# Gated delta-rule mixer: decays of a head loaded ahead into four tiles, two tiles for their exponentials, an output row loaded before its gate's projection, and one small scaling on GpSimd

## The chip, the cores and the metric

The kernel runs on one core of a Trainium2 chip. The metric is the device time of one execution in microseconds (us). Before the change three timed runs took 3221.08, 3230.27 and 3230.47 us, median 3230.27 us; a fourth execution was profiled and took 3224.76 us, of which the span from the first to the last instruction is 3221.8 us. About 0.3% is what a measurement of this kernel can tell from no change.

## The reference, cut to what matters

The model has two layers on 1024 tokens of width 1024. Each has a mixer, a cross attention to 256 memory rows and an MLP. The first layer's mixer is mLSTM and stick-breaking attention; the second layer's mixer, the one changed here, is a gated delta rule with 8 heads of width 128:

```python
qkv, gate, b, a = _split(h @ w_in, C_SIZES)
qkv = jax.nn.silu(short_conv(qkv, conv_w))          # 4 taps
q, k = l2norm(q), l2norm(k)
beta = sigmoid(b); log_alpha = -exp(a_log) * softplus(a + dt_bias)
g = cumsum(log_alpha)                               # inside a chunk
decay = where(incl, exp(g[..., :, None] - g[..., None, :]), 0)
lower = where(strict, beta[..., :, None] * kk * decay, 0)
sol = triangular_solve(lower + eye, rhs)
attn = einsum(q, k) * decay
q_dec = q * exp(g)[..., None]
# then a scan over the chunks with a 128x128 state per head
o = rmsnorm(o, head_gain) * silu(gate)
return o.reshape(B, T, GDN_VW) @ w_out
```

The kernel uses chunks of 128 tokens, so each head has 8 chunks, 4 in each half of the sequence.

## The kernel before, in words

Activations lie feature-major, 128 features by 512 tokens a tile, in two halves of the sequence. Every fp32 matrix product is made of three products of the two fp32r parts of each operand (`mm3`, L156 to L158). A weight tile is loaded (`ldw`, L145), cast on ScalarE (ACT, L149), and its rest is taken on GpSimd (POOL, L150).

The program hands its instructions in the order in which the code makes them; a planner then lays down the order of each engine once, before the run, from its own estimates of times, with earlier code first among what is ready. On the chip each engine works off its list in that order, and so does the SP queue, which issues nearly all DMAs: an instruction that waits holds up all that stand behind it on the same engine. A tile with a tag has `bufs` places; a new tile under a tag waits until its place is free. Places named in `mix_start`'s dictionary (`raw`, `kq`, `vc`, `M`, `qe`, `ua`, `kv`) lie in a pool on the right side of the memory that is closed after the last head's preparation. Five places (tag T) hold all short-lived 128x512 tiles made by `tmp`, two (tag P) the staging tiles.

`mix_c` (L819) is the second layer's mixer. It takes the heads in pairs:

- `gdn_head(h)` (L958) projects k, q and v of the head from the layer's input, six products of 24 matmuls each (`take`, evicted on VectorE (DVE) at L431 into `raw`). Head 0 also makes the gates (`c_gates`, L890), which end with the cumulated decays `gr` in HBM (L956).
- `gdn_pre(h, half)` (L987) follows for each half: convolution and SiLU of the three (L1002 to L1008), transposes of k (L1014), sums of squares on ACT (L1017) and PE (L1022, copied at L1023), the norm factors on DVE and POOL (L1024 to L1029, the power on POOL at L1025), the scaled k (L1031), and at L1033 the factors of q, which `gdn_rec` reads much later. At L1035 to L1037 one tile `M` is taken and the decays of this half's four chunks are loaded into it, the same 512 values on all 128 partitions. ACT makes `qe`, their exponential (L1039); POOL multiplies it by q (L1040) and subtracts the mask from M in place (L1042); ACT takes the exponential of each chunk with a bias (L1045). PE makes the products of k with k and q (L1050), DVE scales them by M into `ua` (L1058), PE transposes v (L1071) and DVE scales it (L1073). The five results go to HBM (`put`, L1088, and L1066).
- `gdn_inv` (L1093) inverts the triangular blocks of a pair: loads at L1103, L1122 and L1123, a long run of small DVE instructions (L1109, L1114), then products at L1129 to L1141.
- `gdn_rec` (L1145) is the recurrence over chunks, for pairs up to head 3, and then for the last four heads together. `gdn_out` normalises a half of a head and, for heads 0 to 3, stores it to `od` (L478).

After that, in the code's order, `c_gate(h)` (L871) projects a head's gate, makes its SiLU (L881, L882) in a staging tile `t`, and for the first four heads multiplies it by the stored output: L884 loads that into `e`, the tile that held the tanh, and L885 multiplies. L886 stores the product. Projections of later heads, gates and memory keys fill PE beside the recurrences.

The part around the decays, in the code before:

```python
M = self.keep("M", dt=F32)
m3 = M.rearrange("p (c t) -> p c t", c=4)
nc.sync.dma_start(out=m3, in_=self.gr[c4, h].partition_broadcast(128))
qe = self.keep("qe", dt=F32)
nc.scalar.activation(qe, M, AF.Exp)
nc.gpsimd.tensor_mul(qe, qe, kq[:, 1])
```

Of the kernel before, what the change touches and what calls it, by code (L numbers as in the profile page):

```python
# [11 lines left out]
F32 = mybir.dt.float32  # L12
# [10 lines left out]
HALVES = (0, 1)  # L23
# [3 lines left out]
class Model:  # L27
# [336 lines left out]
    def mix(self, l):  # L364
        if l == 0:
            with self.phase(
                dict(z=3, so=1, ml=2),
                **dict(kq=8, v=4, e=2, sp=2, sh=2, sl=1, wh=2, wl=1, A=2, ah=1, al=1, so_st=1),
            ):
                self.mix_start(l, "so", dict(M=3, W=2, V=2, N=4, C=1, st=1, gg=1, ot=1))  # L370
                self.mix_ab()
                self.out_parts(False)
                self.x_open(self.x_src)
                self.out_proj(self.a["ab_o"])
        else:
            with self.phase(
                dict(a=2, i=1, rec=2, o=1),
                **dict(X=3, Y=2, Uk=1, pr=1, B=4, y=3, S=4, on=2),
            ):
                self.first = [self.ldw(self.a["c_w"][i]) for i in (8, 0)]  # L380
                self.mix_start(l, "o", dict(raw=5, kq=2, vc=1, M=1, qe=1, ua=1, kv=2))
                self.mix_c()
                self.out_parts(True)
                self.x_open(self.x_src, (1,))
                self.out_proj(self.a["c_o"])
# [214 lines left out]
    def ml_heads(self, p):  # L600
        nc = self.nc
        C = None
        for half in HALVES:
# [3 lines left out]
            for i in range(4):  # L607
# [3 lines left out]

                t = self.keep("M", 512, F32)
                qd, k, q = t[:, :256], t[:, 256:384], t[:, 384:]
                t = self.keep("M", 512, F32)
                vT, d = t[:, :256], t[:, 256:]
# [255 lines left out]
    def c_gate(self, h):  # L871

        nc = self.nc

        def gate(i, w, half):
            cols = slice(half * 512, half * 512 + 512)
            t, e = self.stage(), self.tmp()
            ps = self.proj(w, half)
            with self.tc.high_priority():
                self.scaled(t, ps, half)  # L880
            nc.scalar.activation(e, t, AF.Tanh, scale=0.5)  # L881
            nc.vector.scalar_tensor_tensor(out=t, in0=e, scalar=1.0, in1=t, op0=ALU.add, op1=ALU.mult)  # L882
            if h < 4:
                nc.sync.dma_start(out=e, in_=self.od[h][:, cols])  # L884
                nc.vector.tensor_mul(t, t, e)  # L885
            nc.sync.dma_start(out=self.pj[i][:, cols], in_=t)  # L886

        self.lagged([24 + h], lambda i: self.ldw(self.a["c_w"][i]), gate)
# [69 lines left out]
    def gdn_head(self, h):  # L958

        nc = self.nc  # L960
        raw = {}

        def take(i, w, half):
            t = self.ph2("raw", [128, 515])
            ps = self.proj(w, half)
            with self.tc.high_priority():
                self.scaled(t[:, 3:515], ps, half)
                if half == 0:
                    nc.gpsimd.memset(t[:, 0:3], 0.0)
                else:  # L970
                    nc.gpsimd.tensor_copy(t[:, 0:3], raw[i, 0][:, 512:515])
            raw[i, half] = t
            if (i, half) == (16, 0):
                self.c_gates()

        ld = lambda i: self.first.pop(0) if self.first else self.ldw(self.a["c_w"][i])
        self.lagged((8 + h, h, 16 + h), ld, take, 2 if h == 0 else 1)
        oq = self.cols([128, 8])
        for half in HALVES:
            self.gdn_pre(h, half, [raw[i, half] for i in (8 + h, h, 16 + h)], oq)  # L980
        return oq

    def ph2(self, tag, shape):
        pool = self.pr if tag in self.right else self.ph
        return pool.tile(list(shape), F32, tag=tag, name=self.nm(tag), bufs=self.bufs[tag])

    def gdn_pre(self, h, half, raws, oq):  # L987

        nc = self.nc
        mm = nc.tensor.matmul
        chunks = [slice(i * 128, i * 128 + 128) for i in range(4)]
        c4 = slice(4 * half, 4 * half + 4)
        kq = self.ph2("kq", [128, 2, 512])
        vc = self.keep("vc", dt=F32)
        for tl, raw, dst in zip((8 + h, h, 16 + h), raws, (kq[:, 0], kq[:, 1], vc)):
            cv = self.tmp()  # L1000
            wj = lambda j: self.convw[:, tl * 4 + j : tl * 4 + j + 1]
            nc.scalar.mul(cv, raw[:, 0:512], wj(0))  # L1002
            for j in range(1, 4):
                nc.vector.scalar_tensor_tensor(  # L1004
                    out=cv, in0=raw[:, j : j + 512], scalar=wj(j), in1=cv, op0=ALU.mult, op1=ALU.add
                )
            nc.scalar.activation(dst, cv, AF.Tanh, scale=0.5)
            nc.vector.scalar_tensor_tensor(out=dst, in0=dst, scalar=1.0, in1=cv, op0=ALU.add, op1=ALU.mult)  # L1008
        self.put(h, half, 0, kq[:, 0])

        ss, r, c = (self.small([128, 8]) for _ in range(3))
        pk = self.bank("a")
        for s in chunks:
            nc.tensor.transpose(out=pk[:, s], in_=kq[:, 0, s], identity=self.ident)  # L1014
        kt = self.keep("kv", dt=F32)
        for i, s in enumerate(chunks):
            nc.scalar.activation(kt[:, s], pk[:, s], AF.Square, accum_out=ss[:, i : i + 1])  # L1017
        pn = self.bank("a")
        sq = self.tmp()
        nc.scalar.activation(sq, kq[:, 1], AF.Square)  # L1020
        for i, s in enumerate(chunks):
            mm(pn[:, i : i + 1], sq[:, s], self.ones[:, 0:1], start=True, stop=True)  # L1022
        nc.vector.tensor_copy(ss[:, 4:8], pn[:, 0:4])  # L1023
        nc.vector.tensor_scalar(out=ss, in0=ss, scalar1=0.25, scalar2=EPS, op0=ALU.mult, op1=ALU.add)  # L1024
        nc.gpsimd.tensor_tensor(out=r, in0=ss, in1=self.power, op=ALU.pow)  # L1025
        nc.vector.reciprocal(c[:, 0:4], ss[:, 0:4])
        nc.vector.tensor_mul(c[:, 0:4], c[:, 0:4], self.gcol("beta", h, half))
        kd = c[:, 4:8]
        nc.vector.tensor_mul(kd, c[:, 0:4], self.gcol("ed", h, half))  # L1029
        for i, s in enumerate(chunks):  # L1030
            nc.scalar.mul(kt[:, s], pk[:, s], kd[:, i : i + 1])  # L1031
        self.put(h, half, 3, kt)
        nc.vector.tensor_scalar_mul(oq[:, c4], r[:, 4:8], 0.5 * 128.0**-0.5)  # L1033

        M = self.keep("M", dt=F32)  # L1035
        m3 = M.rearrange("p (c t) -> p c t", c=4)
        nc.sync.dma_start(out=m3, in_=self.gr[c4, h].partition_broadcast(128))  # L1037
        qe = self.keep("qe", dt=F32)
        nc.scalar.activation(qe, M, AF.Exp)  # L1039
        nc.gpsimd.tensor_mul(qe, qe, kq[:, 1])  # L1040
        self.put(h, half, 1, qe)
        nc.gpsimd.tensor_sub(m3, m3, self.mask_a.unsqueeze(1).broadcast_to([128, 4, 128]))  # L1042
        ng = self.gcol("ng", h, half)
        for i in range(4):
            nc.scalar.activation(m3[:, i], m3[:, i], AF.Exp, bias=ng[:, i : i + 1])  # L1045
        ua = self.ph2("ua", [128, 4, 2, 128])
        for i in range(0, 4, 2):
            p = self.bank("a")
            for j in range(2):
                mm(  # L1050
                    p[:, j * 256 : j * 256 + 256].rearrange("p (n t) -> p n t", n=2),
                    kq[:, 0, chunks[i + j]],
                    kq[:, :, chunks[i + j]],
                    start=True,
                    stop=True,
                )
            for j in range(2):
                nc.vector.scalar_tensor_tensor(  # L1058
                    out=ua[:, i + j],
                    in0=p[:, j * 256 : j * 256 + 256].rearrange("p (n t) -> p n t", n=2),  # L1060
                    scalar=c[:, i + j : i + j + 1],
                    in1=m3[:, i + j].unsqueeze(1).broadcast_to([128, 2, 128]),
                    op0=ALU.mult,
                    op1=ALU.mult,
                )
        nc.sync.dma_start(out=self.dense(self.Ud[h])[:, c4], in_=ua[:, :, 0])  # L1066
        self.put(h, half, 2, ua[:, :, 1])

        p = self.bank("a")
        for s in chunks:  # L1070
            nc.tensor.transpose(out=p[:, s], in_=vc[:, s], identity=self.ident)  # L1071
        t = self.keep("kv", dt=F32)
        nc.vector.tensor_mul(  # L1073
            t.rearrange("p (c d) -> p c d", c=4),
            p.rearrange("p (c d) -> p c d", c=4),
            r[:, 0:4].unsqueeze(2).broadcast_to([128, 4, 128]),
        )
        self.put(h, half, 4, t)
# [692 lines left out]
```

## Time and profile before

| what | value |
|---|---|
| timed runs, median (lowest to highest) | 3230.27 us (3221.08 to 3230.47) |
| the profiled execution | 3224.76 us |
| its span | 3221.8 us |
| mean granted TensorE clock | 0.971 |
| PE busy | 3045.2 us, 95% |
| DVE busy | 2115.9 us, 66% |
| ACT busy | 1330.2 us, 41% |
| POOL busy | 945.4 us, 29% |
| DMA | 438.04 MB, mean 136 GB/s |

PE is TensorE's matrix products, DVE is VectorE, ACT is ScalarE, POOL is GpSimd, SP the queue that issues DMAs. "Busy" is the time in which an engine executes an instruction. A wait is put down to what released it last. TensorE's clock has two levels, 1.2 and 2.4 GHz; a granted clock of 1.00 is 2.4 GHz throughout, 0.50 is 1.2 GHz. The stage of the second mixer's head preparations, inversions and first recurrences lies between 1520 and 2010 us of the span, the last recurrences and the gates after it.

### The profile page before, as it was taken

What the parts mean: (1) busy time and instruction counts of PE and PEld (TensorE: products, weight loads), DVE (VectorE), ACT (ScalarE), POOL (GpSimd) and SP (SyncE); (2) the same over time, 40 slices, a digit from 0 to 9 for tenths busy, and PEclk for the clock granted to TensorE, in tenths of its full rate; (3) what the DMA queues carried; (4) which work ended last, traced back from release to release, by engine and by line L of the source; (5) the groups of instructions that cost most, each with busy time, mean ns of one, the idle gap of its engine ahead of it and who ended that gap; (6) DMA issues with size and microseconds to landing.
All of it is one profiled execution on the core that took longest, in us unless ns stands there. A gap on an engine that the chain in (4) does not pass through costs nothing.

```text
span 3221.8 us, 39997 instructions
## 1 busy us (share of the span) xinstructions
PE 3045.2 (95%) x14447; PEld 2511.5 (78%) x14447; DVE 2115.9 (66%) x3342; ACT 1330.2 (41%) x2525; POOL 945.4 (29%) x725
## 2 busy tenths in 40 slices
PE   8999989999899999998988899899999899999997
PEld 6777777888678878887777788788888678878886
DVE  5567475545786667777777775654454786667777
ACT  3254464424354454433443333234333354444442
POOL 2354565313000032234343333125323100023323
PEclk9999989999899999999999899999999999999998
DMA  4333553213244464443345556665212234474432
GB/s 151 109 119 103 156 175 119 70 39 102 75 143 157 152 238 167 147 164 100 87 117 142 149 156 187 191 231 187 66 56 77 97 111 149 157 250 173 148 144 79
DMA packets 268374, 438.04 MB, mean 136 GB/s; under 512 B 38064, under 2 KB 146832, under 8 KB 261008
## 3 DMA queue, kind: packets, MB, share of 16 engines
q1 hardware_dynamic: 268176, 435.50, 41.4%
q8 instruction: 113, 1.85, 0.2%
q14 instruction: 85, 0.70, 0.1%
HBM read 300.60 MB, written 134.81 MB: 135 GB/s over the span
## 4 chain that ended last, share of the span: by engine, by line
PE 33%; DVE 9%; DMA 4%; issue 4%; POOL 1%; ACT 1%; SPq 0%; POOLq 0%; DVEq 0%; ACTq 0%
PE mm L158 3%; PE mm L157 3%; PE mm L156 3%; PE ga L1453 2%; PE ga L1454 2%; PE ga L1455 2%; PE gb L1454 1%; DVE t L1004 1%; PE gb L1455 1%; PE gb L1453 1%; PE gc L1454 1%; PE gc L1455 1%; PE gc L1453 1%; PE mm L1454 1%; PE mm L1455 1%
## 5 line engine op out<-in xcount | busy, mean ns | idle before, releaser
L156 PE MATMUL mm<-hh,wh 128*128 128x512 f32 x1248 | 503.4, 404 | 8.2 <-DVE raw L431 3.5
L157 PE MATMUL mm<-hl,wh 128*128 128x512 f32 x1248 | 504.3, 404 | 0.0
L158 PE MATMUL mm<-hh,wl 128*128 128x512 f32 x1248 | 501.9, 402 | 0.0
L150 POOL TENSOR_TENSOR wl<-wr,wh 128x1024 fp32r<-128x1024 f32 x128 | 320.6, 2506 | 448.8 <-ACT wh L149 423.4
L1445 POOL TENSOR_TENSOR r<-r,r 128x512 f32<-128x512 f32 x64 | 92.0, 1458 | 881.8 <-DVE lo L1412 881.8
L1412 DVE TENSOR_TENSOR lo<-r,hi 128x1024 fp32r<-128x1024 f32 x192 | 252.8, 1317 | 133.1 <-ACT hi L1411 132.3
L1411 ACT CAST hi<-r 128x1024 fp32r<-128x1024 f32 x192 | 201.6, 1051 | 313.7 <-PE mm L1454 126.6
L156 PEld LDWEIGHTS mm<-hh,wh 128*128 128x128 f32 x1248 | 239.4, 192 | 59.2 <-DVE raw L431 4.8
L158 PEld LDWEIGHTS mm<-hh,wl 128*128 128x128 f32 x1248 | 240.5, 193 | 48.3 <-issue 0.9
L157 PEld LDWEIGHTS mm<-hl,wh 128*128 128x128 f32 x1248 | 240.2, 192 | 48.0 <-DVE hl L474 0.4
L149 ACT CAST wh<-wr 128x1024 fp32r<-128x1024 f32 x128 | 133.8, 1046 | 213.2 <-PE mm L157 120.8
L1412 DVE TENSOR_TENSOR lo<-br,hi 128x512 fp32r<-128x512 f32 x224 | 187.0, 852 | 32.9 <-ACT hi L1411 32.8
L1453 PE MATMUL ga<-hi,hi 128*128 128x512 f32 x528 | 206.7, 392 | 1.8 <-ACT w L1550 1.0
L1455 PE MATMUL ga<-hi,lo 128*128 128x512 f32 x528 | 206.5, 391 | 0.0
L1454 PE MATMUL ga<-lo,hi 128*128 128x512 f32 x528 | 206.5, 391 | 0.0
L1411 ACT CAST hi<-br 128x512 fp32r<-128x512 f32 x224 | 133.4, 619 | 152.0 <-PE ga L1455 90.0
L1454 PE MATMUL gb<-lo,hi 128*128 128x512 f32 x432 | 169.8, 393 | 7.6 <-DVE lo L1412 7.6
L1453 PE MATMUL gb<-hi,hi 128*128 128x512 f32 x432 | 169.8, 394 | 3.6 <-ACT hi L1411 3.1
L1454 PE MATMUL gc<-lo,hi 128*128 128x512 f32 x432 | 169.1, 391 | 2.3 <-DVE lo L1412 2.3
L1455 PE MATMUL gb<-hi,lo 128*128 128x512 f32 x432 | 169.0, 392 | 0.0
L1455 PE MATMUL gc<-hi,lo 128*128 128x512 f32 x432 | 168.2, 390 | 0.0
L1453 PE MATMUL gc<-hi,hi 128*128 128x512 f32 x432 | 167.8, 390 | 0.0
(515 smaller groups left out, 7228.5 us busy)
## 6 DMA issues: line engine op xcount, KB each, us to landing
r<-in_w SPq DMA_DIRECT2D x128, 512.0 KB, 4.2
br<-hd SPq DMA_DIRECT2D x56, 1024.0 KB, 5.4
hd<-w SPq DMA_DIRECT2D x160, 256.0 KB, 3.1
B<-Bd SPq DMA_DIRECT2D x64, 384.0 KB, 4.5
hd<-t SPq DMA_DIRECT2D x64, 256.0 KB, 5.2
wr<-in_c_w SPq DMA_DIRECT2D x32, 512.0 KB, 4.3
wr<-in_ab_w SPq DMA_DIRECT2D x24, 512.0 KB, 3.6
pj<-p SPq DMA_DIRECT2D x48, 256.0 KB, 2.1
```

What stands on the lines that cost most here:

```text
L149: nc.scalar.copy(hi, raw)
L150: (eng or nc.gpsimd).tensor_sub(lo, raw, hi.bitcast(F32))
L156: mm(out, w[0], x[0], start=first, stop=False)
L157: mm(out, w[0], x[1], start=False, stop=False)
L158: return mm(out, w[1], x[0], start=False, stop=last)
L1004: nc.vector.scalar_tensor_tensor(out=cv, in0=raw[:, j : j + 512], scalar=wj(j), in1=cv, op0=ALU.mult, op1=ALU.add)
L1411: nc.scalar.copy(hi, src)
L1412: (eng or nc.vector).tensor_sub(lo, src, hi.bitcast(F32))
L1445: self.nc.gpsimd.tensor_add(out[:, i : i + 512], a[:, i : i + 512], b[:, i : i + 512])
L1453: mm(ps, hi, b[k][0], start=first and k == 0, stop=False, skip_group_check=True)
L1454: mm(ps, hi, b[k][1], start=False, stop=False, skip_group_check=True)
L1455: mm(ps, lo, b[k][0], start=False, stop=last and k == 3, skip_group_check=True)
```

## The change

Four things are changed, all in the second mixer. The tile M has 4 places instead of 1 and qe has 2 instead of 1. A new function loads both halves' decays of a head; for heads 1 to 7 it stands at the head's start, ahead of its projections, and for head 0 behind them, since the gates are made there. `gdn_pre` is given its tile and loads nothing. The scaling at L1033 moves from DVE to POOL. In `c_gate` the stored output is loaded into a T tile of its own, ahead of the projection.

```diff
-  self.mix_start(l, "o", dict(raw=5, kq=2, vc=1, M=1, qe=1, ua=1, kv=2))
+  self.mix_start(l, "o", dict(raw=5, kq=2, vc=1, M=4, qe=2, ua=1, kv=2))
...
   def gate(i, w, half):
       t, e = self.stage(), self.tmp()
+      if h < 4:
+          o = self.tmp()
+          nc.sync.dma_start(out=o, in_=self.od[h][:, cols])
       ps = self.proj(w, half)
...
       if h < 4:
-          nc.sync.dma_start(out=e, in_=self.od[h][:, cols])
-          nc.vector.tensor_mul(t, t, e)
+          nc.vector.tensor_mul(t, t, o)
...
   def gdn_head(self, h):
+      if h > 0:
+          M = self.decays(h)
...
       self.lagged((8 + h, h, 16 + h), ld, take, 2 if h == 0 else 1)
+      if h == 0:
+          M = self.decays(h)
       for half in HALVES:
-          self.gdn_pre(h, half, [raw[i, half] for i in (8 + h, h, 16 + h)], oq)
+          self.gdn_pre(h, half, [raw[i, half] for i in (8 + h, h, 16 + h)], oq, M[half])
...
+  def decays(self, h):
+      tiles = []
+      for half in HALVES:
+          tiles.append(self.keep("M", dt=F32))
+          self.nc.sync.dma_start(
+              out=tiles[half].rearrange("p (c t) -> p c t", c=4),
+              in_=self.gr[4 * half : 4 * half + 4, h].partition_broadcast(128),
+          )
+      return tiles
...
-      nc.vector.tensor_scalar_mul(oq[:, c4], r[:, 4:8], 0.5 * 128.0**-0.5)
-      M = self.keep("M", dt=F32)
+      nc.gpsimd.tensor_scalar_mul(oq[:, c4], r[:, 4:8], 0.5 * 128.0**-0.5)
       m3 = M.rearrange("p (c t) -> p c t", c=4)
-      nc.sync.dma_start(out=m3, in_=self.gr[c4, h].partition_broadcast(128))
```

## Rows read from the trace of the kernel before

**Rows 1.** The page, its span and its part 1, busy time of each engine.

```profile
span 3221.8 us, 39997 instructions
...
PE 3045.2 (95%) x14447; PEld 2511.5 (78%) x14447; DVE 2115.9 (66%) x3342; ACT 1330.2 (41%) x2525; POOL 945.4 (29%) x725
```

**Rows 2.** Windows by stage: length, busy per engine (instructions), then granted clock, DMA share, GB/s.

```profile
1520.00:2010.00 490.00, 446.05 (x2334) 373.21 (x2333) 355.21 (x724) 192.20 (x509) 165.31 (x137) 0.95 0.49 136
2010.00:2150.00 140.00, 127.37 (x707) 109.12 (x706) 82.73 (x188) 42.96 (x112) 24.79 (x15) 0.95 0.63 204
```

**Rows 3.** PE's waits, 1530 to 2010 us: in total, times, longest.

```profile
PE a L1050 <- DVE s L1023: 6.6, 4, 3.2
PE a L1050 <- ACT kv L1031: 4.5, 5, 2.5
...
PE a L1071 <- DVE ua L1058: 2.8, 1, 2.8
PE mm L156 <- DVE s L1027: 2.3, 1, 2.3
PE a L1050 <- DVE ua L1058: 2.0, 1, 2.0
...
PE a L1014 <- DVE ua L1058: 0.9, 1, 0.9
```

**Rows 4.** Waits of the other engines, 1530 to 2010 us.

```profile
ACT qe L1039 <- DMA M<-gr: 101.2, 16, 13.0
...
DVE c L1033 <- POOL s L1025: 9.4, 7, 4.2
```

**Rows 5.** Timelines of SP, ACT, DVE and PE around one gap: start, length, and idle before it.

```profile
1626.05 0.74 SPq L1037 DMA_DIRECT2D M<-gr  x1
...
1632.90 0.63 ACT L1039 ACTIVATE qe<-M 128x512 f32<-128x512 f32 x1 [4.60 <-DMA M<-gr]
...
1634.59 0.39 DVE L1024 TENSOR_SCALAR s<-s 128x8 f32<-128x8 f32 x1 [2.76 <-ACT kv L1017]
...
1645.87 0.48 PE L1071 MATMUL a<-ident,vc 128*128 128x128 f32 x1 [2.77 <-DVE ua L1058]
```

**Rows 6.** Windows: one gap (the second row), four stretches behind gaps; columns of rows 2.

```profile
1597.40:1601.20 3.80, 3.80 (x10) 3.03 (x11) 3.18 (x8) 3.22 (x8) 3.13 (x3) 0.55 0.00 0
1642.90:1645.60 2.70, 0.20 (x1) 0.00 (x0) 2.66 (x4) 0.00 (x0) 0.83 (x2) 0.97 0.35 137
1645.60:1649.00 3.40, 3.13 (x10) 2.67 (x11) 2.55 (x6) 2.28 (x4) 0.00 (x0) 0.52 0.00 0
...
1662.70:1666.00 3.30, 3.20 (x8) 2.54 (x9) 3.27 (x15) 0.96 (x4) 1.81 (x3) 0.51 0.01 2
...
1716.30:1720.60 4.30, 3.89 (x10) 2.72 (x11) 4.27 (x12) 3.07 (x7) 1.93 (x4) 0.60 0.21 61
```

**Rows 7.** The load of the decays, L1037: length on SP, first and last start; time to landing.

```profile
L1037 SPq DMA_DIRECT2D M<-gr x16: 383/556/2418, 1555.6 to 1976.8; - x16
...
DMA to landing us min/median/max: 4.7/6.8/8.8
```

**Rows 8.** ACT's timeline at the first head's first half.

```profile
1560.35 0.63 ACT L1039 ACTIVATE qe<-M 128x512 f32<-128x512 f32 x1 [6.07 <-DMA M<-gr]
```

**Rows 9.** Windows: the whole machine between 1580 and 1720 us; columns as in rows 2.

```profile
1580.00:1720.00 140.00, 123.20 (x550) 97.98 (x549) 116.56 (x214) 58.20 (x153) 53.60 (x46) 0.95 0.44 120
```

**Rows 10.** Groups by line, 1530 to 2010 us: busy, mean ns, idle before.

```profile
L1033 DVE TENSOR_SCALAR c<-s 128x4 f32<-128x4 f32 x16 | 8.7, 546 | 11.6 <-POOL s L1025 9.4 <-POOL raw L969 2.2
```

**Rows 11.** Two small POOL operations by line: shortest, median and longest in ns.

```profile
L971 POOL COPY raw<-raw x24: 178/186/691, 1523.7 to 1950.5; 128x3 f32<-128x3 f32 x24
...
L1206 POOL TENSOR_TENSOR s<-s,mhalf x16: 1006/1007/2553, 1879.9 to 2197.9; 128x4 f32<-128x4 f32 x16
```

**Rows 12.** Waits around the gates, 1960 to 2240 us.

```profile
DVE p L885 <- DMA t<-od: 7.0, 6, 2.8
...
DVE p L431 <- DMA pc<-p: 6.5, 3, 4.4
```

More of the change, by code (lines that the diff above doesn't have):

```diff
@@ L985, in ph2, with gdn_pre @@
         return pool.tile(list(shape), F32, tag=tag, name=self.nm(tag), bufs=self.bufs[tag])
-    def gdn_pre(self, h, half, raws, oq):
+    def gdn_pre(self, h, half, raws, oq, M):
         nc = self.nc
```

## The prediction

> **What bounds the kernel now.** I read the page first. PE is busy for 3045.2 of 3221.8 us [rows 1], so whatever the change does elsewhere, it can give back only PE's idle time and the time that PE worked at the lower clock. The windows by stage come next. In the stage of the changed code, 1520 to 2010 us, PE is busy for 446.05 of 490 us at a granted clock of 0.95; behind it, up to 2150 us, for 127.37 of 140 us [rows 2]. So the stage holds 44 us of idle PE and at most another 0.05 x 490 = 24 us of clock. No other engine is full: DVE is busy 355.21 us and ACT 192.20 us of the 490.
>
> PE's own waits tell which part of the 44 us can belong to the change. Six kinds end in work of the head preparation: 6.6 + 4.5 + 2.8 + 2.3 + 2.0 + 0.9 = 19.1 us in 13 waits [rows 3]. The rest belongs to inversions, recurrences and short gaps, which the change doesn't touch directly. The releasers named are DVE and ACT, so I looked at what those waited for. ACT's largest wait is for the load of the decays, 101.2 us in 16 waits, one at each half of each head [rows 4].
>
> One gap shows how the one leads to the other [rows 5]. SP issues the load at 1626.05 us. ACT stands still for 4.60 us until 1632.90. The sums of squares (L1017) stand behind that exponential on ACT, so DVE waits 2.76 us for them before L1024, and everything behind it on DVE comes in a heap: eleven microseconds later PE waits 2.77 us for DVE's `ua`, and during that gap DVE is busy for 2.66 of 2.70 us [rows 6]. Six of the thirteen waits, the long ones, have this pattern of a late load, a standing ACT and then a crowded DVE. Why the load is late is in the code and in its row: there is one tile M, so the load of a half can start only when DVE's L1058 has finished the half before, and from there it takes 4.7 to 8.8 us, median 6.8, to land [rows 7].
>
> A gap costs more than its length. Behind four of these gaps PE worked at the lower level of its clock: granted 0.55, 0.52, 0.51 and 0.60 over 3.8, 3.4, 3.3 and 4.3 us [rows 6], a loss of 1.7 + 1.6 + 1.6 + 1.7 = 6.7 us by length times the missing share.
>
> **The change part by part.** *The decays ahead.* The 16 loads stay, with the same bytes and 16 x 0.56 = 9 us on SP [rows 7]. They move, past the weight loads of the head's projections on SP and past every `put` of the preparation, to the head's start; a place in M is free then, because four places hold two heads and the head before the last has long been finished. They wait for nothing new, except that the first two wait for `gr` as the first one does now. Ahead of a head's preparation PE has 6 x 24 = 144 matmuls, at 446.05 / 2334 = 0.19 us an instruction of this stage [rows 2] some 27 us, three times the longest landing; so the load has landed when ACT comes to it, from head 1 on, and in head 0's second half. The first wait stays, 6.07 us [rows 8]; it costs PE nothing. So about 95 of ACT's 101.2 us go. What PE can get of that is at most the 19.1 us of waits and 6.7 us of clock, 25.8 us, and at least nothing. What is late next is DVE. Between 1580 and 1720 us PE is busy 123.20 and DVE 116.56 of 140 us [rows 9]; if all of PE's 16.8 idle microseconds went, the stretch would last 123 us and DVE would be busy for 95% of it, too much for none of PE's waits to be left. I take somewhat under two thirds, 16 us, since the waits of the pattern are the long ones and all four clock losses follow them.
>
> The Trainium skill ("DMA: Bandwidth & Descriptors", "Anatomy of one DMA") speaks against so large a term: it gives a fixed cost of about 2 us and bytes at 436 GB/s beside it, by which, as an estimate, 256 KB would land in 2.6 us; two thirds of ACT's wait would not exist and the term would be near 5 us. That fit is for DMAs issued from GpSimd, and this load is SP's; the measured 6.8 us [rows 7] decide here.
>
> *The second qe tile.* ACT's next exponential no longer waits for the store of the last. Counted at zero: the halves lie far enough apart, and the store stays hidden under the next half's convolution; without that cover it would be part of ACT's wait above, which is not counted twice.
>
> *The scaling on POOL.* DVE loses 16 instructions, 8.7 us busy, and the 11.6 us for which it stood in front of them until POOL's power was ready [rows 10]: 20.3 us off the engine that is late next. It is what makes the 16 us above believable, and gives PE nothing by itself, as PE never waits for L1033. On POOL the new instruction stands directly behind the power that it reads. Its duration there is not in the trace: 0.19 us is the median of a 128x3 copy, 1.01 us that of a 128x4 power [rows 11], so 3 to 16 us of a stage in which POOL is busy for 165.31 of 490 us [rows 2]. I take the copy's, as a multiplication by a constant is nearest to it. Behind it on POOL wait qe and the masks, by at most 1 us a half. Should POOL hold up DVE while it runs, the upper end would take back most of DVE's gain; that is in the range.
>
> *The output ahead of the gate.* The load no longer waits for the tanh and the product, which both use its tile, and DVE no longer waits for it: 7.0 us in 6 waits before L885 [rows 12]. PE sees little of that. I take 1 us, between 7 us and a loss: the tile is one more of five T places, held over a projection, and if the gates had to wait for places as they now do for staging tiles, that would be another 6.5 us [rows 12] the wrong way.
>
> **The sum.** 16 + 1 = 17 us off the profiled execution's 3224.76 us makes 3207.8 us. The three runs lie from 3.7 us below to 5.7 us above that execution, 2.5 us above it on average, so I predict 3210 us.
>
> **The rivals.** *DVE takes the place (0.18).* The ACT wait goes, but DVE's heap stays, because its work and POOL's stay; PE's gaps keep their number and lose a third of their 19.1 us, the clock drops stay: 6 us gained, 3221 us. For it: DVE is full in the gap [rows 6] and 83% busy around it [rows 9]. Against it: DVE loses 20.3 us and its own wait for ACT.
>
> *PE is put in front of DVE (0.15).* The place is PE's order at L1050, L1071 and L1014. The planner now sees the decays ready early, draws the preparation closer together and puts these products earlier between the projections, where DVE, which runs behind the plan, isn't ready. Each such wait costs about 2 us and 1.7 us of clock [rows 3, 6]. The change loses as soon as there are more of them than the long ones that it removes. With five more long ones than now it is 5 x 3.7 = 18 us slower, 3245 us with the 2.5 us. For it: DVE is the next engine. Against it: it is lightened at the same time.
>
> *The loads don't come earlier on the chip (0.07).* SP works in the planner's order; if the loads stood there behind waiting `put`s, ACT would wait as now, and the time stays near 3227 us. Against it: they stand ahead of the head's projections in the code, and earlier code goes first.
>
> **How the numbers follow.** The forecast has 0.60: nearly all of it is faster by over 0.3%, that is below 3220.6 us. About 0.3% is what a measurement of this kernel can tell from no change. The first and third rivals are no change, 0.18 + 0.07 = 0.25; the second is slower, 0.15. The low end takes the whole 25.8 us and the gates' 7 us, 3224.76 - 32.8 + 2.5 = 3194 us. The high end takes in the two rivals without change and the milder half of the slower one, 3236 us.
>
> **What would show it.** Right: ACT's wait before qe falls from 101.2 to under 15 us; DVE has no wait for the power before a scaling; PE's idle time between 1520 us and the end of the last preparation falls by some 10 us, its waits for the preparation from 19.1 to near 8 us, and one or two fewer stretches at the lower clock stand behind them. Wrong: ACT still waits for M; or it doesn't, and PE's waits at L1050 and L1071 are as many as before; or new waits of PE for recurrences or inversions take their place.

## The result and the profile after

The changed kernel takes 3209.80 us (median of 5 runs, 3203.43 to 3212.15), the kernel before beside it 3229.96 us (median of 5, 3221.08 to 3230.47). The ratio is 0.9943, with a 95% interval of 0.9928 to 0.9958: it is faster, by 18 us of the 3230 as the ratio has it. The profiled execution took 3212.15 us.

The page of the changed kernel, span and part 1, answers to [rows 1]:

```profile
span 3210.4 us, 39963 instructions
...
PE 3036.4 (95%) x14447; PEld 2504.0 (78%) x14447; DVE 2117.5 (66%) x3326; ACT 1332.3 (41%) x2525; POOL 955.1 (30%) x741
```

PE does the same 14447 products in 9 us less busy time (3045.2 us before [rows 1]). For the stages, windows of equal content are better than windows of equal time. The stage of the preparations runs from the end of the gates to the end of the last preparation, 1552 to 2008 us before and 1553 to 1985 us after; then the last inversion, the last recurrences, and the output projection to its end. The kernel before (columns as in [rows 2]):

```profile
1552.00:2008.00 456.00, 414.01 (x2181) 349.71 (x2180) 347.36 (x700) 181.59 (x492) 159.26 (x132) 0.94 0.52 144
2008.00:2116.00 108.00, 99.16 (x550) 85.10 (x549) 61.18 (x136) 25.46 (x61) 18.29 (x11) 0.95 0.56 177
...
1552.00:2320.00 768.00, 708.39 (x3800) 603.02 (x3799) 507.27 (x1017) 294.30 (x745) 264.56 (x190) 0.96 0.53 156
```

The changed kernel, the same stages:

```profile
1553.00:1985.00 432.00, 398.40 (x2127) 335.93 (x2127) 346.52 (x676) 178.69 (x481) 164.25 (x146) 0.96 0.55 149
1985.00:2073.00 88.00, 82.45 (x507) 73.11 (x506) 54.77 (x133) 23.12 (x64) 17.00 (x11) 0.96 0.61 192
...
1553.00:2301.00 748.00, 699.02 (x3798) 594.45 (x3798) 509.38 (x1001) 294.87 (x744) 272.79 (x206) 0.97 0.55 160
```

The mixer as a whole is 20 us shorter, 748 against 768. About half of that is idle PE, 59.6 before (768 - 708.39) and 49.0 after; the other half is the same products (3800 and 3798 recorded) in 9.4 us less, at a granted clock of 0.97 instead of 0.96. The preparations end 24 us sooner after the gates (456 to 432 us) and the last inversion takes 20 us less (108 to 88 us); the work that PE then still has to do takes 24 us more, 228 against 204 us. Outside the mixer the two profiled executions differ the other way, 3221.8 - 768 = 2453.8 us before and 3210.4 - 748 = 2462.4 us after, which is why they lie only 12.6 us apart. Most of that, 7 us, lies behind the mixer, and there it is the profile of the kernel before that is short: its last 3848 products, to the end of the span, take 902.0 us, where the other thirteen profiles of this document have 903.5 to 908.9 us. The mixer itself repeats far better: 768 us in the profile before and in those of two kernels below that gained nothing (the extra memset; the scaling last on DVE).

ACT's waits before the exponential, and the new ones of GpSimd, 1530 to 2010 us of the changed kernel (its L1054 is L1039 of before, L1055 is L1040, L1057 is L1042):

```profile
POOL qe L1055 <- DVE kq L1025: 59.0, 12, 11.2
...
POOL M L1057 <- ACT qe L1054: 45.8, 12, 9.2
ACT qe L1054 <- DMA Bd<-qe: 40.3, 10, 9.8
...
ACT qe L1054 <- DMA M<-gr: 8.5, 2, 6.8
```

The wait for the load has gone from 101.2 us in 16 waits [rows 4] to 8.5 us in 2. A new one stands in its place: ACT waits 40.3 us for a qe tile to be stored, and GpSimd's mask waits 45.8 us behind ACT. GpSimd's wait for this exponential isn't new in itself; before, its product with q (L1040) stood there for longer, in the same window:

```profile
POOL qe L1040 <- ACT qe L1039: 104.3, 8, 23.7
```

In the new order ACT makes the exponential ahead of its use. Its 7th, at 1642.21 us, waits for the store, issued at 1635.50 us, of the 5th qe tile, two halves back; the half whose products PE made just then was the 4th.

PE's waits in the stage of the preparations, changed kernel (L1065, L1086, L1039, L1031 and L1144 are L1050, L1071, L1022, L1014 and L1129 of before):

```profile
PE a L1065 <- ACT kv L1048: 6.7, 5, 2.0
PE i L1144 <- DMA X<-Xd: 6.2, 2, 5.1
PE a L1086 <- DVE ua L1073: 5.7, 3, 3.2
PE rec L1186 <- DVE S L1200: 2.7, 1, 2.7
PE a L1039 <- ACT t L1037: 2.4, 1, 2.4
PE a L1039 <- DVE kv L1088: 2.2, 3, 1.5
PE a L1031 <- DVE ua L1073: 2.0, 2, 1.5
PE a L1065 <- DVE s L1040: 1.4, 1, 1.4
```

Those of the preparation listed here are 6.7 + 5.7 + 2.4 + 2.2 + 2.0 + 1.4 = 20.4 us, against 19.1 us before [rows 3]. The gain is not there.

Where it is shows when the stage is cut in two, at the end of DVE's scaling of the fourth head (L1058, L1073 in the changed kernel). The kernel before, heads 0 to 3 and heads 4 to 7:

```profile
1552.00:1750.00 198.00, 178.05 (x808) 143.93 (x807) 162.79 (x290) 82.67 (x214) 75.86 (x64) 0.95 0.44 118
1750.00:2008.00 258.00, 235.96 (x1375) 205.78 (x1374) 184.56 (x411) 98.92 (x279) 83.39 (x68) 0.94 0.58 164
```

The changed kernel:

```profile
1553.00:1750.00 197.00, 175.18 (x789) 140.51 (x789) 160.47 (x278) 85.94 (x225) 87.75 (x76) 0.96 0.47 124
1750.00:1985.00 235.00, 223.22 (x1339) 195.42 (x1338) 186.04 (x399) 92.75 (x257) 76.50 (x70) 0.97 0.62 169
```

The first four heads, in which the prediction read its gap, gain nothing: 198 and 197 us, though ACT's waits for the load there fell from 42.4 to 8.5 us. All of the gain is in the last four, where PE's idle time falls from 22.0 to 11.8 us and the granted clock rises from 0.94 to 0.97. Of PE's waits there the preparation had only 3.0 us before; it has 0.6 us after. The others, of the inversions and recurrences, fell from 18.7 to 10.9 us.

### The profile page after: what moved, and what is told of

It reads as the page before. It is cut to its first block, busy times and chain, and to the rows that moved or that the text cites. A ratio compares the mean times of both kernels' runs of the same rounds, so it can differ in the third digit from the quotient of the medians.

```text
span 3210.4 us, 39963 instructions
## 1 busy us (share of the span) xinstructions
PE 3036.4 (95%) x14447; PEld 2504.0 (78%) x14447; DVE 2117.5 (66%) x3326; ACT 1332.3 (41%) x2525; POOL 955.1 (30%) x741
```

## The experiments

All were timed in five rounds beside runs of the kernel before on the same chip. Medians of the kernel before were 3224.73, 3224.77, 3225.21 and 3230.68 us in the four groups of experiments and 3229.96 us beside the changed kernel, so ratios are compared and not times. A ratio here isn't the quotient of two medians; the two differ by up to 0.0015, or 5 us (two places each: 0.9901 by the medians), and kernels are told apart no more finely than by their intervals.

| kernel | median us | ratio to before | 95% interval |
|---|---|---|---|
| changed kernel | 3209.80 | 0.9943 | 0.9928 to 0.9958 |
| decays alone | 3214.84 | 0.9963 | 0.9946 to 0.9980 |
| gate alone | 3215.04 | 0.9969 | 0.9954 to 0.9984 |
| scaling alone | 3214.03 | 0.9966 | 0.9952 to 0.9980 |
| changed, one qe tile | 3207.39 | 0.9934 | 0.9915 to 0.9953 |
| before, extra memset | 3223.37 | 0.9997 | 0.9985 to 1.0010 |
| before, scaling last on DVE | 3221.80 | 0.9993 | 0.9980 to 1.0006 |
| before, own tile for the stored output | 3231.83 | 1.0027 | 1.0016 to 1.0038 |
| changed, loads behind the projections | 3204.82 | 0.9940 | 0.9926 to 0.9954 |
| changed, two places for M | 3209.41 | 0.9950 | 0.9933 to 0.9967 |
| changed, one load for all heads | 3190.88 | 0.9896 | 0.9880 to 0.9913 |
| changed, mask in a tile of its own | 3197.24 | 0.9920 | 0.9906 to 0.9935 |
| changed, two places each | 3198.71 | 0.9916 | 0.9891 to 0.9940 |

### Each part alone

**The decays alone.** The gate and the scaling as before:

```diff
-  self.mix_start(l, "o", dict(raw=5, kq=2, vc=1, M=1, qe=1, ua=1, kv=2))
+  self.mix_start(l, "o", dict(raw=5, kq=2, vc=1, M=4, qe=2, ua=1, kv=2))
...
+      if h > 0:
+          M = self.decays(h)
```

> Of the change the decays' part alone: four M tiles, two qe tiles, both loads at the head's start; the scaling stays on VectorE and the gate's load where it was. Theory (the late load of the decays is the cause): ACT's wait for that load falls from 101.2 us to under 15 us and most of the gain is here, some 13 to 20 us below the kernel before (ratio 0.994 to 0.996). Rival (the gain is the scaling's, which frees VectorE, or the gates'): under 6 us gained, ratio above 0.998, though ACT's wait for the load is gone just the same.

Measured: 0.9963, or 12 us. ACT's wait for the load is 9.7 us in 2 waits. Alone, the decays give 12 of the change's 18 us, a little less than expected, and the rival's 6 us lie at the end of the interval. The preparations take 429 us in place of 456, and 14 of these 27 us go again behind them (326 us in place of 312). PE's waits for the preparation stay here as well, 17.2 us in its stage of preparations (1550 to 1979 us): the late load was not what they hung on.

**The gate alone.**

```diff
+  if h < 4:
+      o = self.tmp()
+      nc.sync.dma_start(out=o, in_=self.od[h][:, cols])
   ps = self.proj(w, half)
...
-      nc.sync.dma_start(out=e, in_=self.od[h][:, cols])
-      nc.vector.tensor_mul(t, t, e)
+      nc.vector.tensor_mul(t, t, o)
```

> The gate's part alone: the stored output is loaded into a tile of its own ahead of the gate's projection, all else as before. Theory: VectorE's 7.0 us of waits before the multiplication go, TensorE gets about 1 us, ratio 0.998 to 1.002. Rival (the gates and the end of the mixer carry the gain): 5 us or more, ratio below 0.9985.

Measured: 0.9969, 10 us; the rival. The profiled mixer is 14 us shorter. 8 us of that lie in the stage of the preparations (448 against 456 us), some 3 us of them before 1924 us (the end of DVE's scaling of the 14th half), ahead of the first gate's load at 1955 us. The other 6 us lie behind it. What changes there is seen in SP's own waits, between the end of the last preparation and the end of the last inversion. The kernel before, 2008 to 2116 us:

```profile
SPq L886 <- DVE p L882: 16.2, 4, 7.3
SPq L886 <- DVE X L1114: 10.5, 2, 5.4
...
SPq L884 <- DVE X L1114: 9.0, 2, 6.1
...
SPq L884 <- DVE pr L1109: 5.6, 2, 5.2
SPq L886 <- DVE p L885: 4.5, 2, 3.4
...
SPq L884 <- DMA od<-on: 3.2, 2, 2.2
SPq L886 <- DVE pr L1109: 2.7, 2, 1.4
```

The kernel with the gate's part alone, 1998 to 2087 us (L888 is L886 of before, the store of the gate; L880 is the load):

```profile
SPq L888 <- DVE p L885: 8.3, 3, 4.4
SPq L888 <- DVE p L887: 4.9, 2, 2.7
SPq L888 <- DVE pr L1111: 4.9, 2, 4.3
...
SPq L888 <- DVE X L1116: 3.4, 1, 3.4
...
SPq L880 <- DMA od<-on: 1.6, 1, 1.6
...
SPq L880 <- DMA B<-Bd: 1.1, 1, 1.1
```

Before, SP stood 51.7 us of this stage's 108 in front of a gate's load or store, 17.8 us of it at the loads (L884); with the load ahead it is 24.2 us of 89 by these rows, 2.7 us at the loads (L880). Behind such a waiting DMA on SP stand the loads of the inversion and of the recurrences. SP as a whole is no freer for it: all its waits together take 82 of 108 us before and 68 of 89 us here, 76% both times, and the last experiment of the next section takes as much from the gates' standing without a gain. That the gain comes by SP is argued, not shown. The stage is shorter by 19 us. Part of its filling work is only put off (500 products against 550); up to the end of the output projection the gate's part alone takes 306 us where the kernel before takes 312 (its row stands further down), with PE idle for 13.8 us instead of 17.6 us:

```profile
1998.00:2304.00 306.00, 292.21 (x1623) 251.41 (x1622) 157.60 (x319) 112.26 (x254) 105.30 (x58) 0.98 0.55 175
```

**The scaling alone.**

```diff
-  nc.vector.tensor_scalar_mul(oq[:, c4], r[:, 4:8], 0.5 * 128.0**-0.5)
+  nc.gpsimd.tensor_scalar_mul(oq[:, c4], r[:, 4:8], 0.5 * 128.0**-0.5)
```

> The scaling's part alone: the 128x4 scaling on GpSimd, all else as before. Theory: VectorE loses 20 us of work and waiting, but what TensorE waits for is behind the late load, so the time stays, ratio 0.998 to 1.002. Rival (VectorE is what holds TensorE): 5 us or more gained, ratio below 0.9985. If a new order of the instructions alone moves the time by several us, it shows here too, in either direction.

Measured: 0.9966, 11 us; the rival again. The instruction itself, scaling alone:

```profile
L1033 POOL TENSOR_SCALAR c<-s x16: 229/240/699, 1575.2 to 1986.3; 128x4 f32<-128x4 f32 x16
```

0.24 us on GpSimd is the median; on DVE it is 0.17 us. The mean of 0.55 us [rows 10] comes of a few long ones, up to 3.31 us; of the 8.7 us that the prediction counts as DVE's work, 16 times the median is 2.7 us. DVE's standing of 11.6 us before it [rows 10] is gone. The preparations take 445 us (1549 to 1994) in place of 456, but PE's waits for them stay, 19.4 us.

The three parts alone give 12, 10 and 11 us by their ratios, 33 us together; the change with all three gives 18. They overlap.

### Is it the edit, or any new order?

Three parts of like size, two of them far beyond their working, could be one accident: the planner lays down a new order after any edit. An edit that should do nothing was tried, and two that take a part of the change to pieces.

**An extra memset.** Behind the scaling:

```diff
+  nc.gpsimd.memset(self.small([128, 4], "N"), 0.0)
```

> The kernel before with one small GpSimd memset of 128x4 added in each half's preparation, behind the scaling, which stays on VectorE: GpSimd's side of the moved scaling without VectorE's relief. Theory (each part of the change has its own effect): the time stays or is up to 5 us longer, ratio 0.999 to 1.002. Rival (each part alone gained 10 us only because any edit makes the planner lay out the mixer anew, and the order before is an unlucky one): again some 10 us faster, ratio near 0.9967.

Measured: 0.9997, no change. The stage of the preparations came out as before, 456 us with PE busy 413.56 us:

```profile
1546.00:2002.00 456.00, 413.56 (x2181) 348.89 (x2180) 350.05 (x701) 181.39 (x492) 159.87 (x132) 0.94 0.52 144
```

So not every edit gives 10 us, and one small instruction more on GpSimd costs nothing (unlike the scaling there, it waits for no input). But this edit left the stage nearly as it was; it says little on what an edit that does move the order gives by luck.

**The scaling last, on DVE.**

```diff
-  nc.vector.tensor_scalar_mul(oq[:, c4], r[:, 4:8], 0.5 * 128.0**-0.5)
...
   self.put(h, half, 4, t)
+  nc.vector.tensor_scalar_mul(oq[:, c4], r[:, 4:8], 0.5 * 128.0**-0.5)
```

> The kernel before with the scaling left on VectorE but moved to the end of the preparation, so that VectorE no longer stands before it until the power is ready. Theory (the standing is what the scaling's move took away, not its 2.7 us of work): VectorE's 9.4 us of waits for the power go and the time falls as with the move to GpSimd, 8 to 12 us, ratio near 0.9967. Rival (the relief is in the work or in the new order): under 4 us.

Measured: 0.9993, no change; but the standing it was meant to remove stayed:

```profile
L1078 DVE TENSOR_SCALAR c<-s x16: 149/170/3327, 1568.3 to 1983.9; 128x4 f32<-128x4 f32 x16
...
  POOL s L1025: 10.7, 6
```

DVE still stood 10.7 us for the power in front of the scaling: the planner had put it nearly where it was. The run doesn't tell standing from work, and that question stays open. That a kernel in which DVE wasn't relieved gained nothing fits a gain by DVE's relief, and fits a gain by order alone as well.

**Own tile for the stored output, the load where it was.**

```diff
   if h < 4:
-      nc.sync.dma_start(out=e, in_=self.od[h][:, cols])
-      nc.vector.tensor_mul(t, t, e)
+      o = self.tmp()
+      nc.sync.dma_start(out=o, in_=self.od[h][:, cols])
+      nc.vector.tensor_mul(t, t, o)
```

> The kernel before with the stored output loaded into a tile of its own, the load standing where it stood, behind the gate's SiLU in the code. Theory (in the gate's part the gain is that the load no longer waits on SP for the product that read its tile, so that SP is free for the loads behind it): the planner can place the load early and most of the 10 us of the gate's part are here. Rival (the place in the code, ahead of the projection, is what matters): under 4 us gained.

Measured: 1.0027, slower, by 9 us. The extra tile alone is no gain. The loss is a clock loss. From the end of the last preparation to the end of the output projection, kernel before:

```profile
2008.00:2320.00 312.00, 294.38 (x1621) 253.31 (x1620) 159.91 (x318) 112.71 (x253) 105.30 (x58) 0.97 0.54 174
```

and with the tile of its own:

```profile
2001.00:2322.00 321.00, 306.94 (x1621) 265.49 (x1620) 160.91 (x318) 112.17 (x253) 105.29 (x58) 0.93 0.51 168
```

PE is idle for less, 14.1 against 17.6 us, and yet needs 12.6 us more for the same 1621 products, at a granted clock of 0.93 instead of 0.97. The timed executions agree: the mean granted clock of the twelve is 0.9698, that of the kernel before beside them 0.9715. The loss lies in one stretch of the last inversion; two rows of PE's timeline and a window:

```profile
2047.91 3.44 PE L1130 MATMUL i<-X,Uk 128*128 128x64 f32 x16 [2.68 <-DMA X<-Xd]
...
2081.19 0.77 PE L156 MATMUL mm<-hh,wh 128*128 128x512 f32 x1
```

```profile
2048.00:2082.00 34.00, 33.42 (x152) 32.62 (x153) 12.22 (x25) 8.78 (x28) 4.09 (x4) 0.50 0.49 156
```

PE waits 2.68 us for the inversion's load and then works for 34 us almost without a break at the lower level of its clock. Up to 2081.19 us it has nothing but the small products of the inversion and the recurrences (128x64 and 128x128); from 2083 us, with projections (128x512) beside them again, the clock is 1.00. With the gate's part alone such a stretch lies at 2061 to 2067 us; there the projections come back at 2065.64 us. By length times the missing share the 34 us cost 17 us, an estimate, more than the whole loss.

SP is freed in this kernel nearly as with the gate's part alone: up to the end of the last inversion (2001 to 2103 us) it stands 26.2 us in front of the gates' DMAs and only this at their loads:

```profile
SPq L885 <- DMA od<-on: 0.8, 1, 0.8
```

So the theory's relief came and its gain didn't. Since one stretch of clock outweighs all else, the run doesn't tell either whether the load's place ahead of the projection matters.

### What the decays' part rests on

**One qe tile.**

```diff
-  self.mix_start(l, "o", dict(raw=5, kq=2, vc=1, M=4, qe=2, ua=1, kv=2))
+  self.mix_start(l, "o", dict(raw=5, kq=2, vc=1, M=4, qe=1, ua=1, kv=2))
```

> The changed kernel with one qe tile in place of two. Prediction's step (the second tile costs and gives nothing): time as the changed kernel, within 3 us. Theory after the trace (ACT now waits 40.3 us for the store of an earlier qe tile, 10 times): with one place the wait grows to 70 us or more and half of the gain is lost, 5 to 10 us slower than the changed kernel.

Measured: 0.9934, the same as the changed kernel or a little better. The theory from the trace after fell, its first step already: with one tile ACT's waits for the store are not longer but shorter, 22.6 us in 8. So the second tile buys nothing that can be measured. That ACT's 40.3 us in the changed kernel are no loss is argued from the exponential being made ahead of need; no run here lengthened that wait.

**The loads behind the projections.**

```diff
-  if h > 0:
-      M = self.decays(h)
...
-  if h == 0:
-      M = self.decays(h)
+  M = self.decays(h)
```

> The changed kernel with both loads of the decays at the end of the head's projections for every head, not at its start; four places stay. Theory (the places are what frees the loads, the place in the code matters little as long as it is ahead of the preparation): ACT waits for the load for 10 to 40 us, time within 4 us of the changed kernel. Rival (the distance matters): ACT waits for 60 us or more and the time is 8 us or more above the changed kernel.

Measured: 0.9940, as the changed kernel; ACT waits 9.7 us in 2 waits for the loads, less than expected. No difference shows from the place in the code.

**Two places for M.**

```diff
-  self.mix_start(l, "o", dict(raw=5, kq=2, vc=1, M=4, qe=2, ua=1, kv=2))
+  self.mix_start(l, "o", dict(raw=5, kq=2, vc=1, M=2, qe=2, ua=1, kv=2))
```

> The changed kernel with two places for the decays in place of four: a load then waits until the same half of the head before has been used. Theory (a load is late as soon as its place comes free late): the places of a head come free while the next head is still projected, some 20 us ahead of need, so ACT waits for loads for less than 30 us and the time is within 4 us of the changed kernel. Rival (four are needed): ACT waits for 60 us or more, and half of the decays' gain of 10 us is lost.

Measured: 0.9950, within noise of the changed kernel, though ACT waits for loads again:

```profile
  DMA M<-gr: 58.1, 13
```

Between the two expectations: the waits are back by more than half and the time isn't. Microseconds of ACT's wait are no measure of what they cost. Loads that come a little late, 58.1 / 13 = 4.5 us each and none by more than 6.7 us, cost nothing that can be measured here; the part of the change that took away 101.2 us, with waits of up to 13.0 us, gave 12.

### Further on: the mask

**One load for all heads.** Head 0's tiles serve all heads, and the mask's difference goes to a second tile, W. Left out are the loads of heads 1 to 7 and their right decays (the bias is head 0's too).

```diff
-  self.mix_start(l, "o", dict(raw=5, kq=2, vc=1, M=4, qe=2, ua=1, kv=2))
+  self.mix_start(l, "o", dict(raw=5, kq=2, vc=1, M=2, W=2, qe=2, ua=1, kv=2))
...
-  nc.gpsimd.tensor_sub(m3, m3, self.mask_a.unsqueeze(1).broadcast_to([128, 4, 128]))
+  nc.gpsimd.tensor_sub(m3, w3, self.mask_a.unsqueeze(1).broadcast_to([128, 4, 128]))
```

> The changed kernel without the loads of the decays of heads 1 to 7: all heads use head 0's two tiles, and the mask's difference goes to two tiles of its own, so it overwrites nothing that ACT reads. Left out are the loads and the right decays of heads 1 to 7. Theory (the loads are hidden in the changed kernel): no gain from the missing loads; if anything, some us from the mask that no longer waits for ACT's exponential (GpSimd waits 45.8 us for it now): 0 to 6 us below the changed kernel. Rival (the loads still cost, by the traffic that they put in front of the weights): 8 us or more below the changed kernel.

Measured: 0.9896, 15 us below the changed kernel by the ratios, which is the rival's number. It has two causes in it, the loads and the mask, so the next two runs take the mask alone.

**The mask's difference in a tile of its own**, all loads in place:

```diff
-  self.mix_start(l, "o", dict(raw=5, kq=2, vc=1, M=4, qe=2, ua=1, kv=2))
+  self.mix_start(l, "o", dict(raw=5, kq=2, vc=1, M=4, W=1, qe=2, ua=1, kv=2))
...
-  nc.gpsimd.tensor_sub(m3, m3, self.mask_a.unsqueeze(1).broadcast_to([128, 4, 128]))
+  nc.gpsimd.tensor_sub(m3, w3, self.mask_a.unsqueeze(1).broadcast_to([128, 4, 128]))
```

> The changed kernel with the mask's difference in a tile of its own, one place, so that GpSimd no longer waits for ACT's exponential before it; loads and results as in the changed kernel. Theory (the wait that took the loads' place, 45.8 us on GpSimd and up to 3.2 us at TensorE's transposes behind it): GpSimd's wait goes to under 10 us and the time falls by 2 to 6 us below the changed kernel. Rival (that wait is covered): no change, within 2 us.

Measured: 0.9920, 7 us below the changed kernel by the ratios, a little more than expected, with intervals that just overlap; 26 us below the kernel before. PE's waits in its stage of preparations (1545 to 1965 us; L1087, L1066 and L1145 are L1071, L1050 and L1129 of before):

```profile
PE i L1145 <- DMA X<-Xd: 5.8, 2, 3.3
PE a L1087 <- DVE ua L1074: 4.4, 4, 2.1
PE a L1066 <- DVE s L1040: 2.6, 3, 1.3
PE mm L156 <- DVE raw L431: 2.6, 3, 1.1
PE a L1066 <- ACT kv L1048: 2.2, 1, 2.2
...
PE a L1039 <- ACT t L1037: 1.7, 1, 1.7
PE a L1039 <- DVE kv L1089: 1.1, 2, 0.9
```

and the stage itself:

```profile
1545.00:1965.00 420.00, 395.07 (x2159) 336.74 (x2158) 343.46 (x682) 180.12 (x491) 172.95 (x148) 0.98 0.55 156
```

Here the waits for the preparation did fall, from 20.4 to 4.4 + 2.6 + 2.2 + 1.7 + 1.1 = 12.0 us, the clock rose to 0.98, and the stage lasts 420 us against 432. Nearly all of that is in heads 0 to 3, which take 186 us where they took 198 and 197. GpSimd no longer waits for ACT's exponential; it waits for the place of W instead (59.0 us for DVE's product).

**Two places for the loads and two for the difference**, in the memory of the changed kernel's four, against the kernel with one place for the difference:

```diff
-  self.mix_start(l, "o", dict(raw=5, kq=2, vc=1, M=4, W=1, qe=2, ua=1, kv=2))
+  self.mix_start(l, "o", dict(raw=5, kq=2, vc=1, M=2, W=2, qe=2, ua=1, kv=2))
```

> The changed kernel with two places for the loaded decays and two for the mask's difference, in the memory that the changed kernel gives to four; all loads and results as in the changed kernel. It differs from the kernel without the loads of heads 1 to 7 only in those loads and their values. Theory (the loads are hidden once a place is free in time, and a place now comes free when the mask is taken): as fast as the kernel with one place for the difference or up to 6 us faster, ratio 0.990 to 0.992 against the kernel before, ACT's waits for the loads under 20 us. Rival (the loads cost, as the kernel without them was another 6 us faster): ACT waits for loads for 40 us or more, or SP stands longer, and the ratio stays at 0.992 or above.

Measured: 0.9916, as with one place, ACT waiting 9.7 us in 2 waits for the loads. This kernel differs from the one without loads by the loads and their values alone; 0.9916 (0.9891 to 0.9940) and 0.9896 (0.9880 to 0.9913) overlap: the loads may still cost some 6 us or nothing, which stays open.

## Why the prediction was right, and where not

The time, 3209.80 us against 3210, the sign and the range came out as forecast. Several of the steps didn't, and that the number is met so closely is luck.

- **What bounds the kernel**: right. DVE and ACT are as busy as before, and the time came out of PE's idle time and clock, 10.6 and 9.4 us in the mixer. The clock came out of it nearly as much as the gaps did; I had put 6.7 us of 25.8 there.
- **The load goes off ACT's path**: right, 8.5 us in 2 waits are left. It isn't the head's start that does it, as with the loads behind the projections 9.7 us are left; with two places for M the waits are back at 58.1 us, so the places do count for ACT's wait, though not for the time.
- **Where PE gets it**: wrong. "Its waits for the preparation from 19.1 to near 8 us" is the failing line; they are 20.4 us, and 17.2 us with the decays alone. This comes close to what the prediction called a sign of being wrong: ACT no longer waits for M, and PE's waits at L1050 and L1071 are 9 in place of 11, 13.8 us in place of 15.9. What fell is the other part, which I had set aside as not touched: in the preparations' stage PE's idle time fell from 42.0 us (456 - 414.01) to 33.6 us (432 - 398.40), all of it in the last four heads, while the preparation's waits rose. So inversions, recurrences and short gaps gave it. One gap followed back to the load, in the first four heads, showed what stood before that gap; it didn't show that a gap is gone when the load is early.
- **The decays' 16 us**: 12 alone, with an interval from 6 to 17. The size isn't shown to be off; its way to PE is.
- **The gate's 1 us**: wrong, 10 alone. The working looked at DVE's wait and at a place among the tiles. It left out the moved DMA's queue, where SP stood 51.7 us in front of the gates' loads and stores in the stage of the last inversion, and the order of PE beside that inversion, where one stretch of 34 us at the lower clock made the gate's tile a loss. Which of them gave the 10 us is open.
- **The scaling's nothing**: wrong, 11 alone. "PE never waits for L1033" is true and proves nothing. What it gave isn't PE's waits for the preparation either, 19.4 us in that kernel; the profiled mixer is 9 us shorter, 5 us of it idle PE and 4 us the clock and the same work. By what way DVE's relief leads there is open. Its price on GpSimd, 0.19 us by the copy, was near: 0.24 us where it moved alone.
- **The sum**: 17 us came out right since two terms were far too small and the parts overlap. Sized rightly each, 12 + 10 + 11 = 33 us would have been too much by nearly half.
- **The second qe tile at nothing**: right in time (one tile is as fast), wrong in its reason. The store isn't hidden; ACT waits 40.3 us for it.
- **The rivals**: none came by its time. In heads 0 to 3 the first one's picture did come, PE's waits kept and 1 us gained. But DVE isn't what held these heads: with the mask in a tile of its own they take 186 us with 159.56 us of work on DVE, against 160.47 us in the changed kernel's 197. For the second, PE's waits for the preparation are 15 in place of 13, but none is longer than the longest before (3.2 us both times).

The Trainium skill ("DMA: Bandwidth & Descriptors", "Anatomy of one DMA") would have made the load's term small, by 2.6 us a load. The loads of the changed kernel land in 5.6 to 11.8 us, median 6.5; on the landing the rows decided rightly, and the 5 us of that working lie just under the interval of the decays alone. On the scaling the Trainium skill ("GPSIMD Engine Reference", "Engine selection") sends elementwise multiplications to VectorE: those with two inputs take about twice as long on GpSimd, those with one input run there roughly at line rate. This one has one input tile, and the measured medians lie between the two, 0.24 us against 0.17 us on DVE, on 4 elements a partition. And yet the slower engine made the kernel 11 us faster when this instruction alone moved.

Open is how much of each part's 10 us is its cause and how much a luckier order of the whole mixer: the extra memset moved nothing, but it also left the order nearly untouched.

## What to carry to other kernels

When a part of a change frees an in-order engine or the DMA queue, don't count it at nothing because the busiest engine doesn't name it as releaser; here two parts counted at 0 and 1 us gave some 10 us each, and only trying each alone showed it. Don't add up the parts: three parts of 10 to 12 us made 18. Cut the stage in two before you say where the gain is: here half of the stage that was changed gained nothing. If a wait has been taken away and another stands in its place, look whether anybody needs the result yet: the kernel gained although ACT waits 40.3 us anew, and giving the mask a tile of its own, in place of the one that ACT reads, was worth some 7 us more.

## What the runs showed of the hardware

With the same 1621 products the stage behind the preparations took PE 294.38 us at a granted clock of 0.97 and 306.94 us at 0.93, although PE was idle for 3.6 us less: between two orders of the same work the clock can decide against the idle time. The difference lay in one stretch: behind a gap of 2.68 us PE was busy for 33.42 of 34 us at a granted clock of 0.50, with products of 128x64 and 128x128 alone, and the clock was back at 1.00 two microseconds after products of 128x512 had come back. A 128x4 multiplication by a constant takes 0.24 us on GpSimd (median; 0.17 us on DVE). Outside the mixer, which the change doesn't touch, two profiled executions differ by 8.6 us, nearly half of what was to be measured, while the mixer repeats within 1 us in three kernels of unchanged time.
